# A hybrid encoder layer: x loaded first, modulation sums one block ahead, later transposes of z, another pad order

## The chip, the cores and the metric

The kernel runs on one core of a Trainium2 chip. The metric is device time in microseconds (us) of one launch. Engines are called as in the profile: PE is TensorE's matmul, PEld its weight load, DVE VectorE, ACT ScalarE, POOL GpSimd, SP the engine that issues most DMAs.

## The reference

One layer of an encoder, 512 positions, width 2048, all in float32, cut to what matters:

```python
mod = silu(c) @ w_ada + b_ada                       # 6 x 2048: shift, scale, gate of two sub-layers
sh1, sc1, gt1, sh2, sc2, gt2 = split(mod, 6)
h = rms_norm(x, g_norm1) * (1 + sc1) + sh1
proj = h @ w_in                                      # q, k, v of 8 differential heads, latents of 8 MLA heads
a_out = rms_norm(differential_attention(q, k, v, lam, rel_bias), g_subln) * (1 - lambda_init)
b_out = latent_attention(...)                        # 8 heads of 128
x = x + gt1 * (concatenate([a_out, b_out]) @ w_out)
h2 = rms_norm(x, g_norm2) * (1 + sc2) + sh2
x = x + gt2 * ((silu(h2 @ w_gate) * (h2 @ w_up)) @ w_down)
```

## The kernel before, in words

Every matmul in float32 is made of three (`mm3`, lines 241 to 243): each operand is split in a high and a low part, and high x high, high x low and low x high are summed in PSUM. Of a weight chunk ACT writes the high part (`hi`, L89) and DVE the low one (`lo`, L97); chunks are fetched two ahead (`W.get`).

The first stage forms h transposed, `hT`, one tile of 128 features (a `kc`) at a time, 16 in all, and multiplies it by w_in. The kc are worked in blocks, `BLOCKS` = 2, 2, 4, 4 and 4 of them. In each block five heads come one after the other (`head_block`), each with 12 matmuls of 384 columns for every kc (`ps_in`); after the first block a head's partial sum is added to that of the blocks before on DVE (`raw_in`, L508). For the last block only the first head is done here; the rest is spread as filler over the attention that follows.

Before a block can be multiplied, three things must be there:

- the modulation sums: c times the columns of w_ada that belong to the block, 16 instructions on DVE (`ada_pair`, L334 for the first and L336 for the others; tiles `adaacc`, weights `araw`). A step of the generator `modulation_sums` is two pieces in the blocks of 2 kc and one in those of 4;
- the columns G and SH: PE sums `adaacc` over the partitions (`ps_ada`, L347), DVE reads them out (L348 to 350);
- for each kc, four transposes of the scaled x (`ps_x`, L398), read out by ACT with G and SH as `xt` (L400), then `hh` on ACT (L401) and `hl` on DVE (L402).

While block i is multiplied, `modulation_sums` of block i + 2 (`ahead`) and `modulation` of block i + 1 (`near`) are stepped along with the matmuls. The order of PE is the order in which the code is written. DVE, ACT, POOL and SP run in an order that a scheduler gives them; each takes its instructions in that order.

At the start, SP loads x in 16 tiles with the pieces of block 0 between them, in the order that the string `LOADS` gives (a: two pieces, x: a tile of x, w: the first weight chunk).

The differential heads follow. `DIFF_STEPS` is the order of steps of one head: s scores, t transposes of the probabilities, v values, o and n the next head's operands, F a stretch of filler (in-projection of later heads), e the step `finish` of the head before: four transposes of its normalised tiles z (`ps_zT`, L748). z comes from POOL (L742).

In the down-projection of the feed-forward part (`ps_d`) the hidden activations are split into 32 tiles `ax` of 2 KB a partition. They lie in a pool `fd`, behind a tile `pad` of 32 bytes.

Of the kernel before, what the change touches and what calls it, by code (L numbers as in the profile page):

```python
# [18 lines left out]
P = 128  # L19
# [19 lines left out]
NEAR = 0.2  # L39
LOADS = "aaaxxxxaxxxxaxxxxaxxxxwaa"  # L40
# [158 lines left out]
def hybrid_layer(ctx, tc, a, out):  # L199
# [182 lines left out]
    sums1 = {k0: [] for k0, _ in BLOCKS}  # L382

    def modulation_sums(k0, nk):
        yield from ada_pair(raws0, accs0, 1, 0, k0, nk, sums1[k0])

    def modulation(k0, nk):
# [7 lines left out]
        for kc in range(k0, k0 + nk):  # L395
            ps = bank(spare[0], "ps_x")
            for t in range(NT):
                pe.transpose(ps[:, tsl(t)], xs[t][kc // 4][:, tsl(kc % 4)], ident)  # L398
            xt, hh, hl = slot("xt", F32), slot("hh"), slot("hl")
            act.activation(xt, ps, AF.Identity, scale=G1[:, kc:kc + 1], bias=SH1[:, kc:kc + 1])  # L400
            last_hh[0] = act.copy(out=hh, in_=xt).ins  # L401
            dve.tensor_tensor(out=hl, in0=xt, in1=f(hh), op=ALU.subtract)  # L402
            hT[kc] = (hh, hl)
            yield None

    first = modulation_sums(*BLOCKS[0])
    i = 0
    for kind in LOADS:
        if kind == "a":
            next(first)  # L410
        elif kind == "w":
            W.split(0)
        else:
            t, b = divmod(i, 4)
            sp.dma_start(out=xs[t][b], in_=x[t * P:(t + 1) * P, b * 512:(b + 1) * 512])
            i += 1
# [39 lines left out]
    for t in range(NT):  # L456
        if t % 2:
            act.activation(xs[t][0], xs[t][0], AF.Copy, scale=rstd1[:, t:t + 1])
        else:
            dve.tensor_scalar(out=xs[t][0], in0=xs[t][0], scalar1=rstd1[:, t:t + 1], scalar2=None, op0=ALU.mult)  # L460

# [85 lines left out]
    for gen in (first, modulation(*BLOCKS[0]), modulation_sums(*BLOCKS[1])):  # L547
        for _ in gen:
            pass
    def run(gen, total, at, start, end):  # L550

        n = total * min(1.0, max(0.0, (at - start) / (end - start)))
        while gen[1] < n:
            gen[1] += 1
            next(gen[0], None)

    for i, (k0, nk) in enumerate(BLOCKS):
        final = i + 1 == len(BLOCKS)
        ahead = [modulation_sums(*BLOCKS[i + 2]) if i + 2 < len(BLOCKS) else iter(()), 0]
        near = [iter(()) if final else modulation(*BLOCKS[i + 1]), 0]  # L560
# [927 lines left out]
```

## Time and profile before

| | us |
|---|---|
| median of 3 runs (lowest to highest) | 2285.63 (2285.3 to 2287.18) |
| profiled execution | 2284.71 |
| its span | 2282.9 |
| PE busy in the span | 2194.7 (96%) |
| DVE busy | 1646.3 (72%) |
| ACT busy | 945.1 (41%) |
| mean granted clock of TensorE | 0.989 |

The span runs from the first to the last instruction that the profiler saw. Busy times are of one profiled execution; a matmul's length contains time in which the next one has already begun, so the spacing of starts, and not the length, says what a stream of matmuls costs. A wait is the idle time of an engine just ahead of an instruction, put down to what released it last.

### The profile page before, as it was taken

Reading aid. Unit: us, or ns where it says so; the run is one execution under the profiler, and the core shown is the slowest. Engines: PE = TensorE matmul, PEld = TensorE weight load, DVE = VectorE, ACT = ScalarE, POOL = GpSimd, SP = SyncE. Lnnn points to the kernel's source line nnn. Section 1 sums busy time; section 2 is a strip of 40 time slices with the busy share of each in tenths; the row PEclk is TensorE's granted clock in tenths of the full one; section 3 lists DMA queues with packets and bytes.
Section 4 is the critical chain, followed back from the end, with each engine's and each line's share of the span. In section 5 each row is a group of like instructions: output and inputs, shape, how many; then the busy total and the mean of one; then the engine's idle time right before and its main releaser. Section 6 shows DMA issues by size and latency. Waiting matters only on the chain.

```text
span 2282.9 us, 35317 instructions
## 1 busy us (share of the span) xinstructions
PE 2194.7 (96%) x13878; PEld 2004.6 (88%) x13878; DVE 1646.3 (72%) x2360; ACT 945.1 (41%) x1569; POOL 263.0 (12%) x408
## 2 busy tenths in 40 slices
PE   3899999998989999999999999999999999999999
PEld 2799989997778787899999999999999888888887
DVE  5987787868988686857777777777777676343654
ACT  4423555557555334534444444444444522221221
POOL 0002533436544000000000000000000000000000
PEclk9999999999999999999999999999999999999999
DMA  9975355432433685423333333333333786332442
GB/s 297 322 233 145 90 155 157 131 92 88 162 120 121 214 283 186 135 83 124 121 130 121 121 130 110 122 121 121 112 129 121 253 282 202 101 121 92 157 139 101
DMA packets 270825, 344.99 MB, mean 151 GB/s; under 512 B 15005, under 2 KB 171142, under 8 KB 270530
## 3 DMA queue, kind: packets, MB, share of 16 engines
q1 hardware_dynamic: 267864, 338.18, 45.8%
q10 hardware_dynamic: 2794, 4.55, 0.6%
q8 instruction: 108, 1.77, 0.3%
q14 instruction: 59, 0.48, 0.1%
HBM read 322.71 MB, written 19.96 MB: 150 GB/s over the span
## 4 chain that ended last, share of the span: by engine, by line
PE 68%; DVE 3%; DMA 2%; issue 1%; ACT 0%; POOL 0%; SPq 0%; DVEq 0%; ACTq 0%; POOLq 0%
PE ps_d L243 7%; PE ps_d L242 7%; PE ps_d L241 7%; PE ps_X L1253 5%; PE ps_X L1254 5%; PE ps_X L1255 5%; PE ps_W L1253 3%; PE ps_W L1255 3%; PE ps_W L1254 3%; PE ps_o L241 2%; PE ps_o L243 2%; PE ps_o L242 2%; PE ps_Y L1255 2%; PE ps_Z L1255 2%; PE ps_Z L1253 2%; PE ps_Y L1253 2%
## 5 line engine op out<-in xcount | busy, mean ns | idle before, releaser
L89 ACT CAST hi<-raw 128x1024 fp32r<-128x1024 f32 (+2 forms) x228 | 221.2, 971 | 508.2 <-PE ps_d L242 303.1
L97 DVE TENSOR_TENSOR lo<-raw,hi 128x1024 fp32r<-128x1024 f32 (+2 forms) x215 | 242.7, 1130 | 234.3 <-ACT hi L89 232.4
L1236 ACT CAST wh<-wr 128x1024 fp32r<-128x1024 f32 x160 | 168.6, 1054 | 242.5 <-PE ps_X L1254 68.2
L1254 PE MATMUL ps_X<-comb,wh 128*128 128x256 f32 x960 | 267.9, 279 | 0.0
L1253 PE MATMUL ps_X<-comb,wh 128*128 128x256 f32 x960 | 267.9, 279 | 0.0
L1255 PE MATMUL ps_X<-comb,wl 128*128 128x256 f32 x960 | 267.9, 279 | 0.0
L241 PE MATMUL ps_d<-hi,ax 128*128 128x512 f32 x640 | 253.1, 396 | 0.0
L242 PE MATMUL ps_d<-hi,ax 128*128 128x512 f32 x640 | 253.1, 395 | 0.0
L243 PE MATMUL ps_d<-lo,ax 128*128 128x512 f32 x640 | 253.1, 395 | 0.0
L1219 DVE TENSOR_TENSOR wl<-wr,wh 128x1024 fp32r<-128x1024 f32 x160 | 195.7, 1223 | 73.6 <-ACT wh L1236 73.5
L243 PE MATMUL ps_in<-lo,hh 128*128 128x384 f32 (+2 forms) x704 | 233.1, 331 | 9.8 <-DVE lo L97 9.8
L241 PE MATMUL ps_in<-hi,hh 128*128 128x384 f32 (+2 forms) x704 | 237.9, 338 | 3.4 <-ACT hi L89 2.6
L242 PE MATMUL ps_in<-hi,hl 128*128 128x384 f32 (+2 forms) x704 | 232.3, 330 | 0.8 <-DVE hl L402 0.7
L1236 ACT CAST wh<-wt 128x1024 fp32r<-128x1024 f32 x120 | 126.2, 1051 | 195.6 <-PE ps_X L1254 118.8
L1219 DVE TENSOR_TENSOR wl<-wt,wh 128x1024 fp32r<-128x1024 f32 x120 | 146.8, 1224 | 78.5 <-ACT wh L1236 78.5
L1254 PEld LDWEIGHTS ps_X<-comb,wh 128*128 128x128 f32 x960 | 180.4, 188 | 0.0
L1253 PEld LDWEIGHTS ps_X<-comb,wh 128*128 128x128 f32 x960 | 180.4, 188 | 0.0
L1255 PEld LDWEIGHTS ps_X<-comb,wl 128*128 128x128 f32 x960 | 180.4, 188 | 0.0
L1253 PE MATMUL ps_W<-comb,wh 128*128 128x256 f32 x640 | 179.2, 280 | 0.9 <-DVE cu L1264 0.9
L1254 PE MATMUL ps_W<-comb,wh 128*128 128x256 f32 x640 | 178.6, 279 | 0.0
L1255 PE MATMUL ps_W<-comb,wl 128*128 128x256 f32 x640 | 178.6, 279 | 0.0
L243 PEld LDWEIGHTS ps_in<-lo,hh 128*128 128x128 f32 x704 | 136.5, 194 | 11.4 <-DVE lo L97 11.4
(320 smaller groups left out, 5328.1 us busy)
## 6 DMA issues: line engine op xcount, KB each, us to landing
raw<-in_w_down_dram SPq DMA_DIRECT2D x88, 512.0 KB
araw<-in_w_ada_dram SPq DMA_DIRECT2D x80, 512.0 KB
wr<-in_w_gate_dram SPq DMA_DIRECT2D x40, 1024.0 KB
wr<-in_w_up_dram SPq DMA_DIRECT2D x40, 1024.0 KB
ada<-in_w_ada_dram SPq DMA_DIRECT2D x128, 256.0 KB
raw<-in_w_in_dram SPq DMA_DIRECT2D x128, 192.0 KB
raw<-in_w_out_dram SPq DMA_DIRECT2D x32, 512.0 KB
x<-in_w_ada_dram SPq DMA_DIRECT2D x64, 256.0 KB
```

What stands on the lines that cost most here:

```text
L89: nc.scalar.copy(out=hi[:, :n], in_=raw[:, :n])
L97: e.tensor_tensor(out=lo[:, :n], in0=raw[:, :n], in1=hi[:, :n].bitcast(F32), op=ALU.subtract)
L241: pe.matmul(o, ah, bh, start=start, stop=False)
L242: pe.matmul(o, al, bh, start=False, stop=False)
L243: pe.matmul(o, ah, bl, start=False, stop=stop)
L1219: dve.tensor_tensor(out=out, in0=x, in1=y, op=ALU.subtract)
L1236: act.copy(out=hi, in_=src)
L1253: pe.matmul(ps[bk], wh[:, k], c[:, 0], start=first and k == 0, stop=False, skip_group_check=True)
L1254: pe.matmul(ps[bk], wh[:, k], c[:, 1], start=False, stop=False, skip_group_check=True)
L1255: pe.matmul(ps[bk], wl[:, k], c[:, 0], start=False, stop=k == 7, skip_group_check=True)
```

## The change

It has three parts.

1. *First stage.* All of x is loaded first, then block 0's pieces of w_ada, then the first three weight chunks. The sums of block 0 are done before anything else, its x is transposed before `ps_ada`, and of its two evacuations `hh` is made by ACT and `xt` by DVE, both straight from PSUM. For the later blocks, the table `MODULATE` gives for sums and modulation a start and an end in us of matmul work since the first one, and `run` steps each generator in proportion. So the sums of a block are stepped in the block before it, and its modulation at that block's end; they were stepped two blocks ahead and over the whole block before.
2. *z.* In `DIFF_STEPS` the step e moves from behind the first F to behind "t0 F".
3. *Pad.* The first step of `load_acts(1)`, which allocates `ax`, stands ahead of `pad` now; the pool gives out memory in the order of the requests, so `ax` lies 32 bytes lower.

```diff
-NEAR = 0.2
-LOADS = "aaaxxxxaxxxxaxxxxaxxxxwaa"
+MODULATE = ((0, 2, (0, 0), (0, 0)), (2, 2, (0.0, 13.0), (13.5, 20.0)), (4, 4, (14.0, 36.0), (36.5, 41.5)),
...
+    def evacuate(kc, ps, both):
+        xt, hh, hl = slot("xt", F32), slot("hh"), slot("hl")
+        if both:
+            last_hh[0] = act.activation(hh, ps, AF.Identity, scale=G1[:, kc:kc + 1], bias=SH1[:, kc:kc + 1]).ins
+            dve.tensor_scalar(out=xt, in0=ps, scalar1=G1[:, kc:kc + 1], scalar2=SH1[:, kc:kc + 1], op0=ALU.mult,
+                              op1=ALU.add)
+        else:
+            act.activation(xt, ps, AF.Identity, scale=G1[:, kc:kc + 1], bias=SH1[:, kc:kc + 1])
+            last_hh[0] = act.copy(out=hh, in_=xt).ins
+        dve.tensor_tensor(out=hl, in0=xt, in1=f(hh), op=ALU.subtract)
+        hT[kc] = (hh, hl)
+
+    def turned(kc):
+        ps = bank(spare[0], "ps_x")
+        for t in range(NT):
+            pe.transpose(ps[:, tsl(t)], xs[t][kc // 4][:, tsl(kc % 4)], ident)
+        return ps
...
+    for i in range(16):
+        t, b = divmod(i, 4)
+        sp.dma_start(out=xs[t][b], in_=x[t * P:(t + 1) * P, b * 512:(b + 1) * 512])
...
+    k0, nk, _, _ = MODULATE[0]
+    for _ in modulation_sums(k0, nk):
+        pass
+    spare[0] = "acc"
+    psx = [turned(kc) for kc in range(k0, k0 + nk)]
+    spare[0] = "tmp"
+    W.split(0)
+    W.load(1)
+    W.load(2)
+    ada_columns(sums1[k0], k0, nk, G1, SH1, C_G1, C_BSC1, C_BSH1)
+    for i in range(nk):
+        evacuate(k0 + i, psx[i], True)
+    W.split(1)
...
-    for gen in (first, modulation(*BLOCKS[0]), modulation_sums(*BLOCKS[1])):
-        for _ in gen:
-            pass
...
+    def run(g, at):
+        gen, n, done, (start, end) = g
+        due = n * min(1.0, max(0.0, (at - start) / (end - start)))
+        while g[2] < due:
+            g[2] += 1
+            next(gen, None)
+
+    at = 0.0
+    side1 = [[paced(modulation_sums(k0, nk), 4 * nk + 1, s), paced(modulation(k0, nk), nk + 1, m)]
+             for k0, nk, s, m in MODULATE[1:]]
     for i, (k0, nk) in enumerate(BLOCKS):
         final = i + 1 == len(BLOCKS)
-        ahead = [modulation_sums(*BLOCKS[i + 2]) if i + 2 < len(BLOCKS) else iter(()), 0]
-        near = [iter(()) if final else modulation(*BLOCKS[i + 1]), 0]
...
+            for us in head_block(h, k0, nk, tag):
+                for pair in side1:
+                    for g in pair:
+                        run(g, at)
+                at += us * 1.07
+        while not final and side1 and MODULATE[-len(side1)][0] < BLOCKS[i + 1][0] + BLOCKS[i + 1][1]:
+            for g in side1.pop(0):
+                for _ in g[0]:
+                    pass
...
     side = gate2()
+    more = load_acts(1)
+    next(more)
     pads.append(fd[1].tile([P, 8], F32, name="pad"))
...
-            if b == 0 and i + 1 < n_parts:
+            if b == 0 and 0 < i < n_parts - 1:
                 more = load_acts(i + 1)
...
-DIFF_STEPS = "s0 F e s1 n F t0 F s2 v0 F t1 F s3 v1 F t2 F o0 v2 t3 F o1 v3 F"
+DIFF_STEPS = "s0 F s1 n F t0 F e s2 v0 F t1 F s3 v1 F t2 F o0 v2 t3 F o1 v3 F"
```

At the start, SP's queue before. `xs` is x, `araw` are the pieces of w_ada; the rows ahead of these load four small tiles.

```order
L330 DMA araw<-in_w_ada_dram 128x2x256 x6
L415 DMA xs<-in_x_dram 128x512 x4
L330 DMA araw<-in_w_ada_dram 128x2x256 x2
L415 DMA xs<-in_x_dram 128x512 x4
L330 DMA araw<-in_w_ada_dram 128x2x256 x2
L415 DMA xs<-in_x_dram 128x512 x4
L330 DMA araw<-in_w_ada_dram 128x2x256 x2
```

The same place of SP after (`raw` are the weight chunks of w_in):

```order
L420 DMA xs<-in_x_dram 128x512 x16
L331 DMA araw<-in_w_ada_dram 128x2x256 x16
L78 DMA raw<-in_w_in_dram 128x3x128 x6
L331 DMA araw<-in_w_ada_dram 128x2x256 x4
L78 DMA raw<-in_w_in_dram 128x3x128 x2
L331 DMA araw<-in_w_ada_dram 128x2x256 x6
L78 DMA raw<-in_w_in_dram 128x3x128 x2
```

All 16 tiles of x stand ahead of the first piece of w_ada now, and all 16 pieces of block 0 ahead of the first weight chunk.

On DVE at the end of block 1, before: the adds of a head (L508), the low half of block 2's first weight chunk (`lo_864`, the eleventh low half of the kernel, L97) and, between them, the sums of block 3 (`adaacc_638`, L336).

```order
L508 TENSOR_TENSOR raw_in_543<-raw_in_543,ps_in_786 128x384
L336 SCALAR_TENSOR_TENSOR adaacc_638<-araw_809,c_col_73,adaacc_638 128x1024
L508 TENSOR_TENSOR raw_in_544<-raw_in_544,ps_in_787 128x384
L336 SCALAR_TENSOR_TENSOR adaacc_638<-araw_812,c_col_73,adaacc_638 128x1024
L508 TENSOR_TENSOR raw_in_545<-raw_in_545,ps_in_788 128x384
L336 SCALAR_TENSOR_TENSOR adaacc_638<-araw_838,c_col_73,adaacc_638 128x1024
L508 TENSOR_TENSOR raw_in_546<-raw_in_546,ps_in_789 128x384
L336 SCALAR_TENSOR_TENSOR adaacc_638<-araw_841,c_col_73,adaacc_638 128x1024
L97 TENSOR_TENSOR lo_864<-raw_794,hi_863 128x768
```

The same place after: the adds (L526), the last sums of block 2 (`adaacc_481`, L337), the eleventh low half (`lo_764`, L98), then block 2's columns (L349 to 351) and the first sum of block 3 (`adaacc_843`, L335).

```order
L98 TENSOR_TENSOR lo_719<-raw_674,hi_718 128x768
L337 SCALAR_TENSOR_TENSOR adaacc_481<-araw_737,c_col_73,adaacc_481 128x1024
L526 TENSOR_TENSOR raw_in_485<-raw_in_485,ps_in_714 128x384
L337 SCALAR_TENSOR_TENSOR adaacc_481<-araw_740,c_col_73,adaacc_481 128x1024
L526 TENSOR_TENSOR raw_in_486<-raw_in_486,ps_in_715 128x384
L526 TENSOR_TENSOR raw_in_487<-raw_in_487,ps_in_716 128x384
L526 TENSOR_TENSOR raw_in_488<-raw_in_488,ps_in_717 128x384
L98 TENSOR_TENSOR lo_764<-raw_722,hi_763 128x768
L349 TENSOR_TENSOR G1_93<-ps_ada_786,small_89 128x4
L351 TENSOR_TENSOR SH1_94<-ps_ada_786,small_89 128x4
L350 TENSOR_TENSOR G1_93<-G1_93,small_89 128x4
L335 TENSOR_SCALAR adaacc_843<-araw_844,c_col_73 128x1024
```

The sums that stand among the adds and ahead of the eleventh low half belong to block 2 now, and to block 3 before; of block 3's sums thirteen stood ahead of that low half (L334 once and L336 twelve times), and none does now.

On PE in the third differential head, before: filler (`ps_in`), the transposes of the second head's z (L748), then a step of scores of the third head (`k_3113`, `k_3181`).

```order
L241 MATMUL ps_in<-hi,hh 128x384
L242 MATMUL ps_in<-hi,hl 128x384
L243 MATMUL ps_in<-lo,hh 128x384
L748 MATMUL ps_zT<-anti,z 128x128 x4
L699 MATMUL ps_s<-k_3113,q_3105 128x512
L700 MATMUL ps_s<-klo,q_3105 128x512
L699 MATMUL ps_s<-k_3181,q_3173 128x512
L700 MATMUL ps_s<-klo,q_3173 128x512
```

The same transposes after (L769), with the next step of scores (s2, of the same k) behind them and then values (`ps_z`).

```order
L242 MATMUL ps_in<-hi,hh 128x384
L243 MATMUL ps_in<-hi,hl 128x384
L244 MATMUL ps_in<-lo,hh 128x384
L769 MATMUL ps_zT<-anti,z 128x128 x4
L720 MATMUL ps_s<-k_3113,q_3105 128x512
L721 MATMUL ps_s<-klo,q_3105 128x512
L720 MATMUL ps_s<-k_3181,q_3173 128x512
L721 MATMUL ps_s<-klo,q_3173 128x512
L750 MATMUL ps_z<-v,aTh 128x256 x4
L753 MATMUL ps_z<-v,aTl 128x128 x4
```

Between the old place and the new one there are four score matmuls, 36 matmuls of `ps_in` and four transposes of probabilities (`ps_aT`).

## Rows read from the trace of the kernel before

**Rows 1.** PE's waits over the whole span: total us, times, longest us
```profile
PE ps_ada L347 <- DVE adaacc L336: 32.1, 1, 32.1
PE ps_zT L748 <- POOL z L742: 11.1, 5, 5.6
PE ps_in L243 <- DVE lo L97: 9.8, 4, 5.2
```

**Rows 2.** Windows: length, busy us of PE, PEld, DVE, ACT, POOL, clock, DMA, GB/s
```profile
41.07:207.00 165.93, 152.72 (x837) 147.14 (x838) 137.18 (x192) 63.20 (x96) 4.83 (x7) 0.95 0.80 251
207.00:1000.00 793.00, 760.77 (x4210) 674.26 (x4209) 629.21 (x1193) 393.46 (x863) 254.71 (x391) 0.98 0.46 146
1000.00:2000.00 1000.00, 999.05 (x7628) 956.07 (x7627) 734.82 (x786) 414.23 (x510) 2.05 (x4) 1.00 0.43 141
```

**Rows 3.** Timeline of PE around block 4's start: start us, length us, operation, idle before
```profile
206.08 0.33 PE L241 MATMUL ps_in<-hi,hh 128*128 128x384 f32 x1
...
207.12 0.33 PE L241 MATMUL ps_in<-hi,hh 128*128 128x384 f32 x1
```

**Rows 4.** Timeline of DVE and PE in blocks 1 and 2
```profile
59.06 0.16 DVE L348 TENSOR_TENSOR G<-ps_ada,small 128x2 f32<-128x2 f32 x1 [3.52 <-PE ps_ada L347]
...
111.11 0.95 DVE L97 TENSOR_TENSOR lo<-raw,hi 128x768 fp32r<-128x768 f32 x1
...
112.12 0.69 PE L243 MATMUL ps_in<-lo,hh 128*128 128x384 f32 x1 [5.19 <-DVE lo L97]
```

**Rows 5.** Timeline at the start of the first stage
```profile
29.66 0.63 ACT L453 ACTIVATE sq<-xs 128x512 f32<-128x512 f32 x1
...
34.36 2.32 DVE L336 SCALAR_TENSOR_TENSOR adaacc<-araw,c_col,adaacc 128x512 f32<-128x512 f32 x3
...
41.07 0.69 PE L241 MATMUL ps_in<-hi,hh 128*128 128x384 f32 x1 [0.66 <-ACT hh L401]
...
43.20 0.68 DVE L402 TENSOR_TENSOR hl<-xt,hh 128x512 fp32r<-128x512 f32 x1
```

**Rows 6.** Windows, a stretch of the loading
```profile
20.00:25.00 5.00, 0.00 (x0) 0.00 (x0) 1.50 (x2) 3.54 (x11) 0.00 (x0) 1.00 1.07 371
```

**Rows 7.** Groups of DVE from 30 to 200 us: busy us, mean ns, idle before
```profile
L336 DVE SCALAR_TENSOR_TENSOR adaacc<-araw,c_col,adaacc 128x1024 f32<-128x1024 f32 x45 | 57.6, 1279 | 0.4 <-DMA araw<-in_w_ada_dram 0.2
L97 DVE TENSOR_TENSOR lo<-raw,hi 128x768 fp32r<-128x768 f32 x30 | 28.5, 954 | 10.3 <-ACT hi L89 9.7
L508 DVE TENSOR_TENSOR raw_in<-raw_in,ps_in 128x384 f32<-128x384 f32 x48 | 25.7, 549 | 4.8 <-PE ps_in L243 4.7
L336 DVE SCALAR_TENSOR_TENSOR adaacc<-araw,c_col,adaacc 128x512 f32<-128x512 f32 x19 | 14.2, 750 | 0.5
L402 DVE TENSOR_TENSOR hl<-xt,hh 128x512 fp32r<-128x512 f32 x16 | 11.0, 687 | 2.4 <-ACT hh L401 2.3
```

**Rows 8.** Timeline of POOL and PE at two transposes of z
```profile
318.18 6.69 POOL L666 TENSOR_TENSOR qd<-raw_in,rs 128x256 f32<-128x256 f32 x8
...
329.80 0.47 PE L748 MATMUL ps_zT<-anti,z 128*128 128x128 f32 x1 [5.59 <-POOL z L742]
...
562.25 0.33 PE L748 MATMUL ps_zT<-anti,z 128*128 128x128 f32 x1 [1.75 <-POOL z L742]
```

**Rows 9.** Timeline of PE in the output and the down-projection
```profile
820.20 0.39 PE L241 MATMUL ps_o<-hi,mh 128*128 128x512 f32 x1
...
825.86 0.39 PE L242 MATMUL ps_o<-hi,ml 128*128 128x512 f32 x1
...
2100.01 0.40 PE L243 MATMUL ps_d<-lo,ax 128*128 128x512 f32 x1
...
2106.08 0.40 PE L242 MATMUL ps_d<-hi,ax 128*128 128x512 f32 x1
```

**Rows 10.** Groups of PE over the whole span, by form
```profile
L1254 PE MATMUL ps_X<-comb,wh 128*128 128x256 f32 x960 | 267.9, 279 | 0.0
...
L241 PE MATMUL ps_d<-hi,ax 128*128 128x512 f32 x640 | 253.1, 396 | 0.0
...
L242 PE MATMUL ps_in<-hi,hl 128*128 128x256 f32 x128 | 36.1, 282 | 0.0
```

More of the change, by code (lines that the diff above doesn't have):

```diff
@@ L38 @@
 FIRST = 5
-NEAR = 0.2
-LOADS = "aaaxxxxaxxxxaxxxxaxxxxwaa"
+MODULATE = ((0, 2, (0, 0), (0, 0)), (2, 2, (0.0, 13.0), (13.5, 20.0)), (4, 4, (14.0, 36.0), (36.5, 41.5)),
+            (8, 4, (38.0, 72.0), (73.0, 82.0)), (12, 4, (74.0, 112.0), (113.0, 124.0)))
 BLOCKS = ((0, 2), (2, 2), (4, 4), (8, 4), (12, 4))
@@ L381, in hybrid_layer @@
     last_hh = [None]
-    sums1 = {k0: [] for k0, _ in BLOCKS}
+    sums1 = {m[0]: [] for m in MODULATE}
     def modulation_sums(k0, nk):
         yield from ada_pair(raws0, accs0, 1, 0, k0, nk, sums1[k0])
+    def evacuate(kc, ps, both):
[14 more added lines that the diff above has]
+        return ps
     def modulation(k0, nk):
@@ L395, in modulation @@
         for kc in range(k0, k0 + nk):
[L396 to L403, printed above, removed]
-            yield None
[L406 to L416, printed above, removed]
+            evacuate(kc, turned(kc), False)
+            yield None
+    for i in range(16):
+        t, b = divmod(i, 4)
+        sp.dma_start(out=xs[t][b], in_=x[t * P:(t + 1) * P, b * 512:(b + 1) * 512])
     ps = bank("tmp", "ps_small")
@@ L545, in bias_strips, with paced @@
             sp.dma_start(out=vecd[:, i * 512:(i + 1) * 512], in_=vec[0:H, :])
-    for gen in (first, modulation(*BLOCKS[0]), modulation_sums(*BLOCKS[1])):
-        for _ in gen:
-            pass
[L550 to L555, printed above, removed]
+    def paced(gen, n, span):
+        return [gen, n, 0, span]
+    def run(g, at):
[7 more added lines that the diff above has]
+             for k0, nk, s, m in MODULATE[1:]]
     for i, (k0, nk) in enumerate(BLOCKS):
         final = i + 1 == len(BLOCKS)
-        ahead = [modulation_sums(*BLOCKS[i + 2]) if i + 2 < len(BLOCKS) else iter(()), 0]
-        near = [iter(()) if final else modulation(*BLOCKS[i + 1]), 0]
-        heads = range(1 if final else FIRST)
-        for h in heads:
+        for h in range(1 if final else FIRST):
             tag = next_tag()
             spare[0] = "tmp" if tag == "acc" else "acc"
-            for j, _ in enumerate(head_block(h, k0, nk, tag)):
-                at = (h + j / nk) / len(heads)
-                run(ahead, 16, at, 0.0, 0.9)
-                run(near, 7, at, NEAR, 0.95)
-        for gen in (ahead[0], near[0]):
-            for _ in gen:
-                pass
+            for us in head_block(h, k0, nk, tag):
[7 more added lines that the diff above has]
+                    pass
         if i == 1:
```

## The prediction

> **What bounds the kernel now.** I read the table of PE's waits first. Three entries of it lie where the change acts: one wait of 32.1 us for the modulation sums before the first block, 11.1 us in five waits for a normalised z tile before its transposes, and 9.8 us in four waits for the low half of an input weight [rows 1]. Next the windows. From 41.07 to 207 us (blocks 0 to 3 of the first stage) PE is busy 152.72 of 165.93 us at a mean granted clock of 0.95, and DVE 137.18 us; from 1000 to 2000 PE is busy 999.05 of 1000 us at 1.00 [rows 2]. So the kernel is bound by TensorE nearly everywhere, there is something to take out of the first stage, and in the feed-forward part only a shorter matmul helps.
>
> What should the first stage cost? At the full clock a 384-column matmul starts every (207.12 − 206.08)/6 = 0.1733 us [rows 3]. Blocks 0 to 3 are 5 heads x 12 kc x 12 = 720 of them, 124.8 us; with the small matmuls of the modulation and the transposes (my estimate from the three handovers in the trace: 12 us) 137 us. The stage took 165.9, so up to 29 us are idle time or half clock. A low half that comes late shows where: DVE forms the first one of block 2 at 111.11, and PE, which waits for it, goes on at 112.12 after 5.19 us [rows 4]. On DVE thirteen sums of block 3 stand ahead of it.
>
> The numbers below are against the profiled execution (2284.71 us, 1.8 more than its span), which lies 0.9 below the median.
>
> **First stage.** The change takes no operation away: the same 16 sums a block, low halves and adds stand on DVE. It moves them.
>
> Start: before, the last squares of x begin at 29.66, the last sums of block 0 end at 34.36 + 2.32 = 36.7, the first in-projection matmul starts at 41.07, and the second hl, which the second kc needs, at 43.20 [rows 5]. Ahead of the last tile of x SP had issued 12 of the 16 pieces of block 0. Now x and all 16 pieces go first; the four pieces behind x are 1 MB, at the 371 GB/s of 20 to 25 us [rows 6] 2.8 us. I put the last piece at 32.5 and the last sum at 33.6, 3 us earlier. x is in and scaled long before, and the transposes wait for nothing then. What is late next is the second hl, since the low half of the first weight chunk and two xt now stand on DVE ahead of it: about 42.4, so the second kc gains 1 to 2 us only. The six w_in transfers, issued behind the 16 pieces, are on time for that; were they not, it would cost back these 2 us.
>
> DVE from there: a sum of 512 columns is 0.75 us, of 1024 columns 1.28, a low half 0.95, an add 0.55, an hl 0.69 [rows 7]. The three sums at 34.36 take 2.32 us, 0.77 each [rows 5]; the longer instructions I let start 0.08 us before the one ahead ends, my choice: 1.20, 0.87, 0.46 and 0.61 us. During blocks 0 and 1 DVE does 16 x 0.77 + 16 x 1.20 (sums of blocks 1 and 2) + 10 x 0.87 + 20 x 0.46 + 4 x 0.61 = 51.9 us, more than PE's 240 x 0.1733 = 41.6. In each of blocks 2 and 3 it does 19.2 + 8.7 + 9.2 + 2.4 = 39.5, PE 41.6. (With the full lengths it is 55.7 and 43.6, and the stage ends up to 8 us later.) So DVE sets the start of block 2 and PE what follows: 33.6 + 51.9 + 2 x 41.6 = 168.7. To this come the handovers to blocks 1 to 4: DVE reads the modulation columns only when PE, in its own order, has come to them. The trace shows one such wait, 3.52 us at 59.06, and PE's longest wait in this stage is 5.19 [rows 4]. Four of 3.5 to 5.2 make 183 to 189. After each, PE runs at the lower of its two clock levels for a while (that is what holds the mean at 0.95 [rows 2]), so I take 191 for the start of block 4, which was at 207.12 [rows 3]: **−16**. The bounds: 29 us plus the 1 or 2 of the start, −30, if no handover costs anything; −2, if the handovers eat all but the start. The row that speaks for the middle is the low half at 111.11: with thirteen sums fewer ahead (0.75 + 12 x 1.20 = 15.2 us) and a start 2 us earlier it comes at about 94, and PE reached it at 106.9.
>
> What the order covers it no longer covers: the sums of a block used to be ready a block ahead, and PE's ps_ada waited for nothing. Now DVE has no lead. A wait of DVE on ps_ada holds the low halves, hl and adds behind it, and PE waits for those.
>
> **Transposes of z.** Of the 11.1 us in five waits [rows 1] the longest is the fourth z tile at 329.80, 5.59 us, while POOL runs eight qd for 6.69 us ahead of that z [rows 8]. The new place is 4 score matmuls, 36 of 384 columns and 4 transposes later: 36 x 0.1733 alone is 6.2 us, more than any of the waits. POOL's order stays. The wait at 562.25, 1.75 us [rows 8], belongs to the last head, whose step stands elsewhere. Removable: 11.1 − 1.75 = 9.35; I take **−9**. Low end −5 (half comes back as a wait for the high and low parts of z, which are made later now and are read only by the output projection much later), high end −11.
>
> **The pad.** Nothing waits less there; what changes is addresses. In the memory map of the built programs the 32 tiles ax, stationary operand of the down-projection, start 32 bytes past a multiple of 64 before and on one after; its moving operand (hi, lo) starts on one in both. Matmuls of 512 columns with both operands 32 past (the output projection) start every (825.86 − 820.20)/25 = 0.2264 us; with one on the line and one 32 past, as the down-projection now, every (2106.08 − 2100.01)/26 = 0.2335 [rows 9]. There are 3 x 640 with ax [rows 10]: 1920 x 0.0071 = 13.6 us, if equal placement is what makes the difference. I take **−12**. Bounds: 0, if it is not, and −18, if both on the line beats both past it. Against: among 256-column matmuls the lengths are 279 ns with the operands placed differently (ps_X) and 282 with both 32 past (ps_in) [rows 10], so there the equal placement is not the shorter.
> The Trainium skill speaks against this term: "TensorE: Matmul & The Clock Gate", section "Step-by-step: what each phase is for", says that weights and the streamed operand come through two independent read ports and that loading the next weights takes nothing from the running matmul. By that rule two placements could not differ and the term would be 0. The 0.2264 and 0.2335 of the trace do differ, whatever their cause, and both are above the 216 ns that the page gives for an isolated 512-column matmul.
>
> **Sum**: 2284.71 − 16 − 9 − 12 = 2247.7; I say 2248.
>
> **Rivals.**
> 1. *The placement does nothing.* The two spacings differ because the one runs with a busier DVE and ACT, or for another property of the tiles. For it: the 256-column rows. Against: the spacing is the same over stretches of 25 matmuls with no wait in them. Time: 2284.7 − 16 − 9 = 2260. The Trainium skill's rule above would give the same.
> 2. *The first stage gains only its start and a little.* The wait removed at 112 comes back at the starts of blocks: each handover costs about 7 us instead of 4 (ps_ada, columns, transposes, evacuation, then hl behind sums). The first stage gives −5: 2258.7. For it: DVE's 51.9 us against PE's 41.6 in blocks 0 and 1. Against: low halves and hl stand earlier in DVE's order. With rival 1 as well: 2271.
> 3. *Slower.* DVE without a lead gates every block's start; while PE waits, nothing else of it is ready, and its clock falls each time. With −21 from the other two parts this decides only if block 4 starts after 228, that is at handovers of (228 − 168.7)/4 = 15 us, three times the longest wait of the stage. At 16 us each, block 4 starts at 233 and the time is 2284.7 + 26 − 21 = 2290.
>
> **How the numbers follow.** Forecast 0.5, its own range 2240 to 2257 (first stage −10 to −22, z −7 to −10, pad −10 to −14). Rival 1 0.2, rival 2 0.19, both together 0.07, rival 3 0.04. The 8-in-10 range takes in rivals 1 and 2 and part of both together: 2236 to 2268. A difference under 0.2% (4.6 us) can't be told from none; slower by more holds rival 3, 0.04; within it what is left of the mixed cases, 0.03; faster 0.93.
>
> **What would show it.** First stage: block 4's first matmul near 191; the first low half of block 2 near 94; waits of PE on ps_ada, hl or lo at four block starts of 3 to 5 us each, and a mean clock of about 0.95. If they are 7, rival 2. Transposes: the entry for z in PE's waits falls from 11.1 to about 2. Pad: the spacing of the ps_d matmuls, 0.2265 in place of 0.2335, and with it 4.5 us for each line's 640; if it stays at 0.2335, rival 1. The forecast as a whole is wrong if the time is above 2257, or if a part of the kernel that none of these touches has moved by more than 3 us.

## The result, and the profile after

| | before | changed |
|---|---|---|
| median of 4 runs, us (lowest to highest) | 2286.4 (2285.3 to 2287.22) | 2255.85 (2254.86 to 2259.78) |
| ratio, 95% interval | | 0.987 (0.9853 to 0.9887) |
| profiled execution, us | 2284.71 | 2256.41 |

The change takes 30.5 us off; 38 were forecast (2248 after 2285.63). It is within the range of the likeliest case (2240 to 2257), near its end; the same kernel in a later run had 2260.77, outside it. In the two profiled executions the difference of the spans is 28.3 us, and the starts of like matmuls say where it lies. The five columns lie between marks: from the span's start to the first in-projection matmul, from there to block 4 (the first stage's blocks 0 to 3), from block 4 to the gate and up projections (the attention heads and what follows them, called the heads below), these projections, and from the start of their last matmul to that of the last of all.

| us | start | blocks 0 to 3 | heads | gate and up | down |
|---|---|---|---|---|---|
| before | 41.07 | 166.04 | 790.15 | 786.02 | 494.52 |
| changed | 36.91 | 155.35 | 789.31 | 786.09 | 481.83 |

The first two columns together gave 14.9 us (forecast 16), the heads 0.8 (forecast 9), the down-projection 12.7 (forecast 12). So the forecast stands in two of its parts, and the third, the gain in the heads, is nearly gone in this execution.

PE's waits over the span of the changed kernel, which answer to [rows 1] (the wait of 17.2 us for ps_x, at the start, is left out here):

```profile
PE ps_ada L348 <- DVE adaacc L337: 10.7, 2, 9.9
PE ps_in L243 <- DVE hl L397: 4.3, 5, 1.6
...
PE ps_z L753 <- DVE aTl L629: 3.6, 3, 2.9
PE ps_in L244 <- DVE lo L98: 3.6, 4, 1.9
PE ps_aT L743 <- DVE cf L729: 3.5, 1, 3.5
...
PE ps_zT L769 <- POOL z L763: 1.8, 1, 1.8
```

The wait for z fell from 11.1 to 1.8 us, the one at the last head, as forecast. The waits of the in-projection for lo fell from 9.8 to 3.6, none over 1.9; those for hl rose from 0.7 to 4.3, two of them (1.6 and 1.1) right at the start of the stage. New are the ones for aTl (3.6, the low part of the transposed probabilities) and cf (3.5, a factor that scales the probabilities pm before they are transposed), both in the differential heads.

The windows, with the same columns as [rows 2]:

```profile
36.91:192.00 155.09, 146.26 (x834) 139.72 (x835) 136.97 (x193) 61.67 (x94) 0.53 (x1) 1.00 0.85 268
192.00:1000.00 808.00, 775.21 (x4347) 688.24 (x4346) 645.63 (x1210) 401.11 (x874) 256.81 (x397) 0.98 0.46 148
1000.00:2000.00 1000.00, 998.43 (x7583) 956.98 (x7582) 731.89 (x785) 413.62 (x509) 2.05 (x4) 1.00 0.43 142
```

Blocks 0 to 3 take 155.09 us now with PE busy for 146.26 and the clock at 1.00; they took 165.93 with 152.72 and 0.95. So 4.4 us of the gain are idle time and 6.4 are matmuls that run faster. Where some of the time of before lay is shown by a window of the kernel before, right behind the wait for the low half, [rows 4]:

```profile
112.00:116.00 4.00, 3.88 (x12) 3.89 (x13) 4.00 (x6) 0.00 (x0) 0.00 (x0) 0.50 1.07 329
```

There the granted clock is 0.50, the lower of the two levels, with PE busy all the time. In the changed kernel, a stretch from early in block 2 to near the end of block 3, and one in the heads that the next part speaks of:

```profile
100.00:190.00 90.00, 89.46 (x528) 86.65 (x526) 80.05 (x114) 30.25 (x42) 0.11 (x1) 1.00 0.78 244
372.40:380.00 7.60, 7.60 (x31) 7.57 (x32) 7.25 (x17) 2.66 (x8) 2.34 (x4) 0.62 0.81 229
```

From 100 to 190 us PE is busy 89.46 of 90 us at the full clock: no handover costs an idle microsecond there (0.54 us in all).

The start, which answers to [rows 5]:

```profile
21.91 11.77 DVE L337 SCALAR_TENSOR_TENSOR adaacc<-araw,c_col,adaacc 128x512 f32<-128x512 f32 x15
...
33.73 1.86 PE L348 MATMUL ps_ada<-ones,adaacc 128*128 128x1 f32 x8 [9.91 <-DVE adaacc L337]
...
36.91 0.69 PE L242 MATMUL ps_in<-hi,hh 128*128 128x384 f32 x1 [1.32 <-ACT hh L391]
...
40.87 0.68 DVE L397 TENSOR_TENSOR hl<-xt,hh 128x512 fp32r<-128x512 f32 x1
...
42.10 0.52 PE L244 MATMUL ps_in<-lo,hh 128*128 128x384 f32 x1
...
42.42 0.52 PE L242 MATMUL ps_in<-hi,hh 128*128 128x384 f32 x1
```

The sums of block 0 end at 33.7 (33.6 forecast), the first matmul comes at 36.91 and the second hl at 40.87 (42.4 forecast). The rows of DVE and PE behind, which answer to [rows 4] and [rows 3]:

```profile
61.18 0.16 DVE L349 TENSOR_TENSOR G<-ps_ada,small 128x2 f32<-128x2 f32 x1 [2.63 <-PE ps_ada L348]
...
92.87 0.95 DVE L98 TENSOR_TENSOR lo<-raw,hi 128x768 fp32r<-128x768 f32 x1
...
192.26 0.42 PE L242 MATMUL ps_in<-hi,hh 128*128 128x384 f32 x1
```

DVE's wait at the columns of block 1 is 2.63 us (3.52 before). From the end of block 0's sums to block 2's first low half, 33.68 to 92.87, DVE is busy 51.18 of 59.19 us, and 51.9 were forecast. Block 2's first low half comes at 92.87 (111.11 before, about 94 forecast), and block 4 starts at 192.26 (207.12 before, 191 forecast).

The transposes of z of [rows 8] in the changed kernel: POOL's eight qd, the fourth z, and PE.

```profile
303.07 7.80 POOL L687 TENSOR_TENSOR qd<-raw_in,rs 128x256 f32<-128x256 f32 x8
...
315.35 0.40 POOL L763 TENSOR_TENSOR z<-z,zs 128x128 f32<-128x128 f32 x1
...
317.43 0.60 PE L769 MATMUL ps_zT<-anti,z 128*128 128x128 f32 x4
```

The z is done at 315.75, 1.7 us before PE comes to it. And the down-projection, which answers to [rows 9, 10]:

```profile
2069.29 0.39 PE L244 MATMUL ps_d<-lo,ax 128*128 128x512 f32 x1
...
2075.18 0.39 PE L243 MATMUL ps_d<-hi,ax 128*128 128x512 f32 x1
```

```profile
L242 PE MATMUL ps_d<-hi,ax 128*128 128x512 f32 x640 | 249.0, 389 | 0.0
```

26 steps in 5.89 us are 0.2265 us (0.2335 before), and each line's 640 matmuls take 249.0 us (253.1 before).

### The profile page after: what moved, and what is told of

The parts are those of the page before. It is cut to its first block, busy times and chain, and to the rows that moved or that the text cites. A ratio compares the mean times of both kernels' runs of the same rounds, so it can differ in the third digit from the quotient of the medians.

```text
span 2254.6 us, 35313 instructions
## 1 busy us (share of the span) xinstructions
PE 2174.1 (96%) x13878; PEld 1994.9 (88%) x13878; DVE 1647.6 (73%) x2362; ACT 943.6 (42%) x1567; POOL 260.8 (12%) x408
## 4 chain that ended last, share of the span: by engine, by line
PE 65%; DVE 2%; DMA 1%; issue 0%; ACT 0%; POOL 0%; SPq 0%; DVEq 0%; ACTq 0%
PE ps_d L243 7%; PE ps_d L242 7%; PE ps_d L244 7%; PE ps_X L1275 5%; PE ps_X L1276 5%; PE ps_X L1274 5%; PE ps_W L1274 3%; PE ps_W L1275 3%; PE ps_W L1276 3%; PE ps_o L244 2%; PE ps_o L242 2%; PE ps_o L243 2%; PE ps_Z L1275 2%; PE ps_Y L1275 2%; PE ps_Z L1276 2%; PE ps_Y L1276 2%
## 5 line engine op out<-in xcount | busy, mean ns | idle before, releaser
L98 DVE TENSOR_TENSOR lo<-raw,hi 128x1024 fp32r<-128x1024 f32 (+2 forms) x215 | 242.7, 1129 | 220.7 <-ACT hi L90 219.3
L244 PE MATMUL ps_d<-lo,ax 128*128 128x512 f32 x640 | 249.0, 389 | 0.0
L243 PE MATMUL ps_d<-hi,ax 128*128 128x512 f32 x640 | 249.0, 389 | 0.0
L242 PE MATMUL ps_d<-hi,ax 128*128 128x512 f32 x640 | 249.0, 389 | 0.0
L244 PEld LDWEIGHTS ps_d<-lo,ax 128*128 128x128 f32 x640 | 120.1, 188 | 25.0
```

What stands on the lines that cost most here:

```text
L98: e.tensor_tensor(out=lo[:, :n], in0=raw[:, :n], in1=hi[:, :n].bitcast(F32), op=ALU.subtract)
L242: pe.matmul(o, ah, bh, start=start, stop=False)
L243: pe.matmul(o, al, bh, start=False, stop=False)
L244: pe.matmul(o, ah, bl, start=False, stop=stop)
```

## The experiments

Two theories on the heads stood at the start: A, that the new waits for aTl and cf come from the earlier first stage, and B, that they are the price of z's new place. On the first stage: C, that the order of the sums on DVE brings the gain, and D, that loading x first does. Beside each median stands that of the kernel before, run along with it on the same chip; the latter lies between 2283.2 and 2289.2 us, and its single runs between 2281.4 and 2292.7. So a stage is best read in the profiles, of which there is one for each line. All of them, by the marks of the table above:

| us | median | that of before | start | blocks 0 to 3 | heads | gate and up | down |
|---|---|---|---|---|---|---|---|
| old place of z | 2265.50 | 2287.31 | 37.69 | 155.87 | 792.85 | 790.95 | 481.82 |
| the same again | 2262.87 | 2286.39 | 36.78 | 155.38 | 792.19 | 791.72 | 481.82 |
| changed, again | 2260.77 | 2286.39 | 38.00 | 156.47 | 785.94 | 789.60 | 483.80 |
| only z | 2282.44 | 2287.31 | 41.16 | 165.18 | 788.84 | 785.21 | 494.53 |
| only pad | 2274.94 | 2287.31 | 41.23 | 164.04 | 788.96 | 788.79 | 481.84 |
| only x first | 2287.11 | 2287.31 | 38.31 | 168.12 | 789.59 | 789.13 | 494.51 |
| less side work | 2259.68 | 2289.17 | 36.72 | 160.40 | 788.21 | 785.67 | 482.01 |
| z behind s2 | 2258.79 | 2289.17 | 38.26 | 156.61 | 786.25 | 789.01 | 481.82 |
| weights 32 past | 2293.89 | 2289.17 | 41.18 | 165.73 | 789.99 | 807.61 | 482.30 |
| ax 16 past | 2282.70 | 2289.17 | 41.16 | 166.63 | 792.84 | 790.61 | 492.12 |
| wh, wl 16 past | 2268.44 | 2283.19 | 37.00 | 156.72 | 783.33 | 795.45 | 489.44 |
| x last | 2263.54 | 2283.19 | 40.10 | 156.85 | 789.32 | 789.19 | 481.83 |

Where the operands lie as before, the gate and up projections take 785.2 to 791.7 us, with the same code: some 6 us between executions that no part of the change makes.

**z at its old place in the changed kernel.**

```diff
-DIFF_STEPS = "s0 F s1 n F t0 F e s2 v0 F t1 F s3 v1 F t2 F o0 v2 t3 F o1 v3 F"
+DIFF_STEPS = "s0 F e s1 n F t0 F s2 v0 F t1 F s3 v1 F t2 F o0 v2 t3 F o1 v3 F"
```

> The changed kernel with the z transposes back at their old place (the first of the three parts and the third remain). In the changed kernel PE's position gained 9 us by about 392 us of the kernel before (offset of like matmuls from -15 to -23.3), and lost it again: a wait of 2.92 us for aTl at 372.31 with a stretch at a granted clock of 0.62 behind it, and one of 3.48 for cf at 536.04. Theory A: those losses come from the earlier first stage (the loads of the gate's columns of w_ada are not in time for DVE), not from z's new place; then the new place is worth its 9 us and this kernel takes about 2256 + 9 = 2265 us, with the waits for aTl and cf still in it. Theory B: the losses are the price of z's new place (the reading out of ps_zT on DVE now falls among the work that aTl queues behind); then the two waits are gone here, the waits for z are back, and the time is about 2256, within 2 us.

Measured: 2265.5 us, ratio to the kernel before 0.9907 (0.9892 to 0.9922). By the time alone that is theory A. PE's waits say B:

```profile
PE ps_zT L769 <- POOL z L763: 11.2, 5, 5.7
...
PE ps_aT L743 <- DVE pm L734: 2.0, 1, 2.0
```

The five waits for z are back, the waits for aTl (0.2 us now) and cf are gone. The heads take 792.85 us, 3.5 more than in the first profile of the changed kernel; of the 9.65 us between the medians of the two kernels 4.9 are in the gate and up projections.

**Only z's new place in the kernel before.**

> The kernel before with the new place of the z transposes alone. Theory A: 2286.4 - 9 = 2277 us, PE's waits for z fall from 11.1 to about 2 us and no new wait of over 1 us appears. Theory B: 2284 to 2287, with new waits of PE for aTl, cf or pm of some 6 us in all in the differential heads.

Measured: 2282.44 us, ratio 0.9979 (0.9969 to 0.9989), between the times of the two theories. Its waits:

```profile
PE ps_z L732 <- DVE aTl L608: 4.0, 3, 3.2
PE ps_aT L722 <- DVE cf L708: 3.5, 1, 3.5
...
PE ps_zT L748 <- POOL z L742: 1.8, 1, 1.8
```

The two new waits are here without the earlier first stage, 3.2 us at the longest. So theory A falls: they belong to z's new place. The gain, 4.9 us by the medians, 1.3 us in the heads of the two profiles, is less than the 9.35 of the waits removed, and the new ones take 7.5, with 0.8 more for another aTl.

**z one step later still.**

```diff
-DIFF_STEPS = "s0 F s1 n F t0 F e s2 v0 F t1 F s3 v1 F t2 F o0 v2 t3 F o1 v3 F"
+DIFF_STEPS = "s0 F s1 n F t0 F s2 e v0 F t1 F s3 v1 F t2 F o0 v2 t3 F o1 v3 F"
```

> The changed kernel with the z transposes one step later still, behind the scores s2. Theory F (the read-out of ps_zT on DVE at the new place delays aTl of the next step): the read-out falls behind the work on s2 now, the wait for aTl at 372 changes by over 1 us and the kernel by 3 us or more either way. Theory E (gate sums and their loads): the wait at 372 stays, the time is 2256 within 2 us.

Measured: 2258.79 us, the same as the changed kernel within what runs differ. The wait for aTl at 372 (here 370.93) fell from 2.92 to 0.27 us, as F says and E doesn't; the kernel did not move, as E says. So neither holds whole. The wait itself, and PE's waits for aTl over the span:

```profile
370.93 0.33 PE L753 MATMUL ps_z<-v,aTl 128*128 128x128 f32 x1 [0.27 <-DVE aTl L629]
```

```profile
PE ps_z L753 <- DVE aTl L629: 2.6, 4, 1.7
...
PE ps_z L750 <- DVE aTl L629: 1.1, 1, 1.1
```

By 378 us PE was 4.1 us ahead of the changed kernel, by 504 only 0.3. Its heads take 786.25.

**Less side work in the fourth head.** What DVE and PE do in the changed kernel at that wait:

```profile
366.77 0.75 DVE L309 SCALAR_TENSOR_TENSOR ada<-ada,c_col 128x512 f32<-128x512 f32 x1 [0.95 <-DMA ada<-in_w_ada_dram]
...
368.58 0.75 DVE L309 SCALAR_TENSOR_TENSOR ada<-ada,c_col 128x512 f32<-128x512 f32 x1 [0.99 <-DMA ada<-in_w_ada_dram]
...
370.04 0.75 DVE L734 SCALAR_TENSOR_TENSOR pm<-pm,cf 128x512 f32<-128x512 f32 x1
370.70 0.95 DVE L98 TENSOR_TENSOR lo<-raw,hi 128x768 fp32r<-128x768 f32 x1
371.57 0.69 DVE L629 TENSOR_TENSOR aTl<-ps_aT,aTh 128x512 fp32r<-128x512 f32 x1
...
372.31 0.90 PE L753 MATMUL ps_z<-v,aTl 128*128 128x128 f32 x3 [2.92 <-DVE aTl L629]
```

DVE waits twice for a load of w_ada, and the pm, the lo and the aTl queue behind.

```diff
-DIFF_SIDE = (1, 2, 1, 2, 1, 2, 1, 1)
+DIFF_SIDE = (1, 2, 1, 1, 1, 2, 1, 1)
```

> The changed kernel with one step fewer of the side work (the sums for the gate's columns of w_ada, which DVE takes in its queue) in each stretch of filler of the fourth differential head: third number after the first of DIFF_SIDE 2 becomes 1; the rest is done later. In the changed kernel PE waits 2.92 us for aTl at 372.31 there; ahead of that aTl DVE sits idle 0.95 and 0.99 us for loads of w_ada. Theory E: it is those sums and their late loads that hold aTl; then the wait falls below 1 us, PE's position behind it is 4 to 6 us earlier, and the time about 2251 us unless the postponed sums give the wait back in a later head. Theory F: the wait comes from the read-out of ps_zT at its new place; then it stays within 0.5 us of 2.92, and the time at 2256.

Measured: 2259.68 us, by the time as F says. The 2.92 is gone, as E says, and one of 2.08 stands at the aTl before:

```profile
366.42 0.39 PE L750 MATMUL ps_z<-v,aTh 128*128 128x256 f32 x1 [2.08 <-DVE aTl L629]
```

Behind both PE had caught up 4.5 us on the changed kernel, and from 393 to 470 us, where the postponed sums run, it lost 5.8 again. Both theories have a part: what holds aTl is DVE's queue, of which late gate sums are one piece and the read-out of ps_zT another. To name shares is not possible from these runs. Its blocks 0 to 3, which the edit does not touch, took 160.40 us; the clock in them was 0.96, against 1.00 in the first profile of the changed kernel.

**The changed kernel and the one with z at its old place once more, side by side.**

> The changed kernel once more, on the same chip and in the same rounds as the next one. Up to the feed-forward part the two profiles of the changed kernel and of the one with z at its old place differ by 4.8 us (first matmul of the gate and up projections at 981.57 and 986.41), their medians by 9.65; the rest lies in the length of the gate and up projections, 786.1 against 791.0 us, which no part of the change touches. If that length varies from run to run, this kernel comes out at 2256 to 2260 and its gate and up projections anywhere from 785 to 791 us.

> The changed kernel with z at its old place once more. If z's new place is worth what the profiles show ahead of the feed-forward part, some 5 us: 2261 to 2264 where the run above has 2256 to 2259. If it is worth its whole 9 us: 2265 or more beside 2256.

Measured: 2260.77 (2253.94 to 2261.61) and 2262.87 (2261.93 to 2266.18); their medians differ by 2.1 us only, and the first lies just above its forecast. The gate and up projections took 789.6 and 791.7 us in the profiles, so their length does vary.

The heads took 792.85 and 792.19 us with the old place. With the new one, and otherwise the same code in the heads, there are four profiles: besides the two of the changed kernel those with wh and wl 16 past and with x last (both below). Each can be taken apart in PE's idle time, the time at the lower clock level by the trace's records of the granted clock, and a rest that is the heads less the idle time less half the time at the lower level:

| us | heads | PE idle | at the lower level | rest |
|---|---|---|---|---|
| old place | 792.85 | 33.9 | 37.6 | 740.2 |
| old place, again | 792.19 | 34.5 | 34.1 | 740.7 |
| changed | 789.31 | 32.8 | 30.7 | 741.2 |
| changed, again | 785.94 | 33.3 | 20.5 | 742.5 |
| wh, wl 16 past | 783.33 | 30.3 | 23.9 | 741.1 |
| x last | 789.32 | 33.7 | 27.3 | 742.0 |

The means are 792.5 and 787.0. So z's new place is worth about 5.5 us behind the new first stage, with a spread of up to 4 either way. The rest lies between 739.8 and 742.5 us in all fourteen profiles. PE's idle time falls by 1.7 us only, because other waits came in for those for z; the time at the lower level falls by 10, which is worth 5. That time also differs by 10 us between the two profiles of the changed kernel, so most of this gain hangs on something that varies from one execution to the next.

The first stage shows the same. In the second profile of the changed kernel, the stage and a stretch right behind a wait in it:

```profile
90.48 0.66 PE L244 MATMUL ps_in<-lo,hh 128*128 128x384 f32 x1 [1.86 <-DVE lo L98]
```

```profile
38.00:194.47 156.47, 148.49 (x837) 142.28 (x838) 137.41 (x194) 61.92 (x94) 0.53 (x1) 0.98 0.84 264
90.60:93.80 3.20, 3.20 (x10) 3.20 (x11) 3.20 (x5) 0.00 (x0) 0.00 (x0) 0.50 0.65 171
```

Behind that wait the lower level stands. In the first profile the wait is there too, and the higher level behind it:

```profile
88.75 0.45 PE L244 MATMUL ps_in<-lo,hh 128*128 128x384 f32 x1 [1.88 <-DVE lo L98]
```

**Only the pad.**

> The kernel before with the ax tiles allocated ahead of the pad alone. In the changed kernel the ps_d matmuls with ax start every 227 ns instead of 233.5. If the placement does that by itself: 2286.4 - 13 = 2273 us, ps_d at 227 ns and everything ahead of the down-projection unchanged. If it took the other parts too (another phase of the DMA or of DVE): 2286, ps_d at 233.5.

Measured: 2274.94 us, ratio 0.9945 (0.9933 to 0.9958), and the down column falls from 494.52 to 481.84. This part of the change does it by itself; that it is the placement, and not the earlier request, the next run shows.

**Weights 32 past a multiple of 64.** `padw` is a list like `pads`.

```diff
         fw.append(open_pool("fw"))
+        padw.append(fw[0][1].tile([P, 8], F32, name="padw"))
```

> The kernel before with a tile of 32 bytes allocated first in the pool of the feed-forward weights: the streamed operand of ps_d starts 32 bytes past a multiple of 64 now, as its stationary operand ax does, and in the gate and up projections the stationary operand wh and wl moves to 32 past as well, where the streamed operand comb is already. Theory G (equal places make a 512-column matmul shorter): ps_d starts every 227 ns in place of 233.5, as in the changed kernel, though ax hasn't moved: -13 us in that stage. Theory H (it is the stationary operand's own start that counts): ps_d stays at 233.5. For the 256-column matmuls of the gate and up projections (6720 of them, 117 ns on average before, operands at different places): the 372 matmuls of the kernel before that have both operands 32 past start every 120 ns; if that is their placement, +20 us here, and the whole kernel is slower by 7; if equal places were better there too, -13 or more, and the kernel ends near 2260.

Measured: 2293.89 us, ratio 1.0026 (1.0014 to 1.0037). The order of the requests for ax is that of before. Two groups of this kernel, to set beside [rows 10]:

```profile
L1254 PE MATMUL ps_X<-comb,wh 128*128 128x256 f32 x960 | 271.7, 283 | 0.0
...
L241 PE MATMUL ps_d<-hi,ax 128*128 128x512 f32 x640 | 249.0, 389 | 0.0
```

The length of ps_d falls from 396 to 389 ns, and its starts are 226.7 ns apart, though ax hasn't moved: theory G, and not the place of one operand. The 256-column matmuls went the other way: from 279 to 283 ns in length, all but a few of the 6720 with 120 ns from start to start, and 807.61 us in place of 786.02. Both their operands are 32 past here; with both on a multiple of 64 they were not run, so for this width equal places and wh's own place are not told apart.

**ax 16 past, in the kernel before.** `load_acts(1)` steps ahead of the pad as in the change, and each ax is used from its byte 16 on.

```diff
-                ah, al = [fd[1].tile([P, S], F32R, tag="ax", bufs=32, name="ax") for _ in range(2)]
+                ah, al = [fd[1].tile([P, S + 16], F32R, tag="ax", bufs=32, name="ax")[:, 4:4 + S] for _ in range(2)]
...
```

> The kernel before with ax allocated ahead of the pad and 64 bytes longer, and used from its byte 16 on: every ax starts 16 bytes past a multiple of 64, the streamed operand on one. If the two starts must be at the same place within 64 bytes: 233.5 ns from start to start in ps_d, or more. If only the half of 64 bytes counts in which each start lies: 227 ns.

Measured: 232.2 ns from start to start in ps_d (the mean of the middle 80%, 233.4 before and 226.7 in the changed kernel); down 492.12. That is far from the 227 of the theory that only the half of 64 bytes counts, and 1.2 below the 233.4 that the other gives. (The profiled execution, of 2290.26 us, is the longest of eight; by the medians this kernel is 6.5 us faster than before, of which its down-projection explains 2.4.)

**wh and wl 16 past, in the changed kernel.** Each tile is 64 bytes longer.

```diff
-        hi, lo = [fw[0][1].tile([P, 8, P], F32R, tag=n, bufs=W_BUFS, name=n) for n in ("wh", "wl")]
+        hi, lo = [fw[0][1].tile([P, 1040], F32R, tag=n, bufs=W_BUFS, name=n)[:, 4:1028].rearrange(
+            "p (a b) -> p a b", a=8) for n in ("wh", "wl")]
...
-                t = fw[0][1].tile([P, 8, P], F32R, tag="w" + kind[0], bufs=W_BUFS, name=kind)
+                return fw[0][1].tile([P, 1040], F32R, tag="w" + kind[0], bufs=W_BUFS, name=kind)[:, :1024]
             return t.rearrange("p a b -> p (a b)")
```

> The changed kernel with the stationary tiles wh and wl of the gate and up projections used from byte 16 on: they start 16 bytes past a multiple of 64, where they started on one; the streamed comb stays 32 past, and the down-projection keeps its places. With 32 bytes between the two the 6720 matmuls of 256 columns took 785 to 791 us (spacings of 113 to 120 ns mixed), with equal places 807.6 (120 ns all through). Theory J (only whether the places are equal counts): 785 to 791 again, the kernel at 2256. Theory K (what counts is the distance, and 16 bytes are between 0 and 32): 795 to 800 us, the kernel at about 2266. Theory L (a smaller distance than 32 that is not 0 is best): under 780 us, the kernel under 2250.

Measured: 2268.44 us; gate and up 795.45 us, theory K, in one profile and 3.7 us above the longest with the old places. The down-projection was meant to keep its places and slowed to 489.44 us: its moving tiles still start on a multiple of 64, but each is 64 bytes longer, so that they lie 4160 and not 4096 bytes apart, and ps_d starts every 230.5 ns (middle 80%):

```profile
L243 PE MATMUL ps_d<-hi,ax 128*128 128x512 f32 x640 | 252.4, 394 | 0.0
```

So to start at the same place within 64 bytes is not the whole rule; what the whole rule is stays open.

**Only x first.** In the kernel before:

```diff
-LOADS = "aaaxxxxaxxxxaxxxxaxxxxwaa"
+LOADS = "xxxxxxxxxxxxxxxxaaaaaaaaw"
```

> The kernel before with only the order of the first loads changed: all 16 tiles of x, then block 0's pieces, then the first weight chunk; sums of the other blocks as before, two blocks ahead. In the changed kernel the first matmul of the in-projection came 4.2 us earlier and block 4 started 14.8 us earlier. Theory C: the stage is limited by DVE's order (thirteen sums of block 3 ahead of block 2's first low half); then the early start is worth at most its 3 to 4 us and the wait near 112 us stays: 2283 us, block 4 at 203 to 204. Theory D: the early start is what brings the gain, since all of DVE's queue follows from it: 2272 us, block 4 near 192.

Measured: 2287.11 us, ratio 0.9999 (0.999 to 1.0008). The start is 2.8 us earlier, at 38.31, block 4 starts at 206.43, and the wait of before stands where it stood:

```profile
111.89 0.69 PE L243 MATMUL ps_in<-lo,hh 128*128 128x384 f32 x1 [5.08 <-DVE lo L97]
```

Theory C, though not its number (block 4 at 203 to 204): of the 2.8 us at the start only 0.7 are left at block 4.

**x last, in the changed kernel.** The loop of `modulation_sums` of block 0 moves ahead of the loads of x:

```diff
+    k0, nk, _, _ = MODULATE[0]
+    for _ in modulation_sums(k0, nk):
+        pass
     for i in range(16):
...
-    k0, nk, _, _ = MODULATE[0]
-    for _ in modulation_sums(k0, nk):
-        pass
```

> The changed kernel with the first loads turned round: block 0's 16 pieces of w_ada before x, their sums on DVE while x comes in; all else as changed. Theory C (the gain of the first stage comes from the sums standing one block ahead on DVE, not from x): the first in-projection matmul is as late as before the change, 40 to 41 us, but block 4 starts at 192 to 195, as DVE has block 0's sums behind it earlier; 2256 to 2259 us. Theory D (x first brings it): block 4 at 200 or later, 2264 us or more.

Measured: 2263.54 us, ratio 0.9902 (0.9882 to 0.9922). The first in-projection matmul and the first of block 4:

```profile
40.10 0.69 PE L242 MATMUL ps_in<-hi,hh 128*128 128x384 f32 x1 [1.32 <-ACT hh L391]
...
196.95 0.42 PE L242 MATMUL ps_in<-hi,hh 128*128 128x384 f32 x1
```

Blocks 0 to 3 take 156.85 us, as in the changed kernel, though x comes last; block 4 starts 4.7 us later than in the changed kernel, of which 3.2 are the start. Block 4 and the time lie between what C and D forecast; the stage's length says C. So the new order in the stage gives it its 10 us, and only with it does the earlier start come through to block 4. The order is that of the sums and of the modulation behind them, which the table `MODULATE` sets together, with block 0's new evacuation; no run takes these apart, and that the sums are the cause rests on the thirteen fewer ahead of block 2's first low half and its coming when forecast.

## Why the prediction was right, and where not

- *The start* came as worked out: sums at 33.7 for 33.6, the w_in transfers in time; the second hl was 1.5 us earlier than forecast.
- *DVE's queue as the bound up to block 2* held: 92.87 for about 94, with DVE busy 51.18 us for the 51.9 of the sum. With x last the stage is as short, and with x first alone as long as before: it is the order on DVE that counts, and not x. Rivals 2 and 3, in which the order gains little or loses, are out.
- *Handovers*: the term was right in its sum and wrong in its kind. "Four of 3.5 to 5.2" were to be waits; PE's longest wait behind the start is 1.9 us, for a low half, and from 100 to 190 us PE is idle 0.5 us in all. From the low half at 92.87 to block 4 at 192.26 are 99.4 us. PE ran 492 matmuls of the in-projection in them, 85.3 us at 0.1733; its small matmuls took 10.7, which the sum of 168.7 left out, idle time 1.0, and the slower ones among the 492 the other 2.4. That 183 to 189 came out near is luck in this: waits that were not there stood for work that was not counted.
- *The clock*: "after each, PE runs at the lower of its two clock levels" did not hold in the first profile of the changed kernel (1.00 over the stage, as far as it is recorded) and held for two waits of the second (0.98 over the stage, 0.50 behind the wait of 1.86 us). It holds for before, where 0.50 follows the wait of 5.19 us, and in the changed kernel behind the wait of 2.92 at 372 (0.62). Over the seven profiles with the new stage unaltered the lower level takes 0 to 13.7 us of it (mean 5.4), over the five with the old one 10.2 to 20.5 (mean 16.4); PE's idle time is 8.4 against 13.7. So faster matmuls made some 5.5 us of the gain (6.4 in the first pair), which the forecast had inside its sum but not as a term.
- *z*: the step that failed in size. Of the 9.35 us removable all went, and the price "half comes back as a wait for the high and low parts of z" was looked for at the wrong tile. It is DVE's queue that pays: with the transposes of z at their new place PE waits 2.9 us for aTl and 3.5 for cf, which come from DVE; with the old place it does not. −9 measured −0.8 in the first pair of profiles, −5.5 over all beside the new first stage, −1 to −5 without it; and most of the 5.5 is time at the lower clock level, not waits.
- *The first stage's gain is not kept whole*: block 4 starts at 192.2 to 197.1 us in the seven profiles with the new stage unaltered (mean 194.0), and at 205.3 to 207.8 in the five with the old one (mean 206.7). With z at its old place the heads then take 792.5 us, where with the old first stage they take 789.0 to 792.8 (mean 790.3 of five, only x first among them). Some 2 us may go there; with two profiles against five that differ by 3.9 among themselves it is not shown.
- *The pad*: 12.7 us for 12, and rival 1 is out: ps_d starts every 226.7 ns in place of 233.4 when ax moves by 32 bytes, and also when its moving operand does. The 256-column matmuls rose from 116.7 to 120.0 ns by the second of these. So relative placement counts, with a sign that differs by width, and the lengths of 282 ns for ps_in against 279 for ps_X, which the prediction put down as evidence against, fit that. Why placement counts is not shown. The Trainium skill, "TensorE: Matmul & The Clock Gate", section "Step-by-step: what each phase is for", has loading the next weights take no read bandwidth from the running matmul, which leaves no room for a difference by placement there; the measurement, 226.7 against 233.4 ns, decides.
- Summed over what the runs give for each part: 12.7 at block 4, 5.5 in the heads and 12.7 in the down-projection, together 30.9, or some 29 if 2 go in the heads, of the 30.5 measured.
- One of the prediction's signs could not have told anything: "a part of the kernel that none of these touches has moved by more than 3 us". The gate and up projections differ by 6 us between executions without any change to them.

## What to carry to other kernels

When a sum or a preload stands far ahead of its use in an engine's queue, look at what queues behind it: here its early place cost more than its lateness would have, and part of that cost was the clock behind a wait. A wait that is taken out by moving work to a later place has to be priced on the engine that reads the moved work out, too. Where waits and the lower clock level come together, take a stage apart into idle time, time at the lower level and rest, and look at several profiles of the same kernel before a few microseconds are put down to a change. Before a stream of many matmuls, try the start addresses of both operands, for each width apart, and compare the spacing of starts.

## What the runs showed of the hardware

- Spacing against placement of both operands in SBUF, at the higher clock: 512 columns 226.7 ns with equal places (both on a multiple of 64, or both 32 past) and 233.4 with 32 bytes between them modulo 64, 232.2 with 16; 256 columns 120.0 with equal places (both 32 past), 117.8 with 16, 116.7 to 117.3 with 32. Where tiles lay 4160 bytes apart, 512 columns took 230.5 with equal places modulo 64.
- Behind the first matmul the changed kernel's 384-column matmuls start every 0.32 us, 42.10 and 42.42 in the rows above, up to 46.90 us. That is the step of the window from 112 us of before too, 12 in 3.88 us, where the granted clock reads 0.50. The windows of the start read 1.00 all the same: the trace's records of the granted clock begin at 47.1 us (at 49.6 in the kernel before).
- The time at the lower level differs between executions of the same kernel: in the two profiles of the changed kernel 0 and 6.8 us of the recorded part of the first stage, and 30.7 and 20.5 us of the heads.
- The same gate and up projections, with the same places, took 785.2 to 791.7 us from execution to execution, with the spacings between 113 and 120 ns in other shares each time.
